# Gated outputs split where they are made, sigmoids loaded a job ahead, adaLN sums in another order, results stored one at a time

## The chip, the core and the metric

The kernel runs on one core of a Trainium2 chip. Its time is the device time in microseconds (us) of one execution. The engines that matter are TensorE (PE in the profile, with its weight loads as PEld), VectorE (DVE), ScalarE (ACT), GpSimd (POOL) and SyncE (SP). SP does no arithmetic: it issues every transfer between the chip's memory and the core's on-chip tiles, one after the other from one queue. A transfer that has to wait for its data holds all transfers behind it in that queue.

## The reference

One layer of a hybrid decoder block over 2048 tokens with 1024 channels, in fp32. What is computed:

```
ada = silu(c) @ w_ada + b_ada;  shift, scale, gate = split(ada)
h = rms_norm(x, g_pre) * (1 + scale) + shift
pv, pg, hq, hf, hi, hg, mg_pool, mg_hgrn = split(h @ w_in)        # 1024 -> 7168
P = per_group_linear(trailing_mean(pv) - pv) * pool_scale * silu(pg)   # 4 groups of 128 channels
A = P @ w_pool_o                                                      # 512 -> 1024
f = lb + (1 - lb) * sigmoid(hf);  q = silu(hq);  k = 1 - f;  v = hi
S_t = diag(f_t) S_(t-1) + k_t v_t^T;  o_t = S_t^T q_t                 # 8 heads of 128 channels
G = rms_norm(o, hgrn_norm_g) * silu(hg)
B = G @ w_hgrn_o                                                      # 1024 -> 1024
merged = sigmoid(mg_pool) * A + sigmoid(mg_hgrn) * B
out = x + gate * rms_norm(merged @ w_out, g_post)
```

P and G are the "gated outputs" of the title; the two sigmoids of the merge are the "sigmoids".

## The kernel before

**Products.** Every fp32 operand of a large matrix product is held as two fp32r tiles: hi is a cast of the value (ACT), lo is the value minus hi (DVE). A product is three matmuls, hi·hi, hi·lo and lo·hi (`three`, L275; all of them are recorded at L273). The helper that makes the two is `split` (L168, L169).

**Order of work.** The tokens are done in two passes of 1024, each as two halves t of 512. A pass is:
1. h, transposed to channels by tokens (`h_in`, L437), and the V projection in jobs (`v_job`, PSUM tiles psV). In pass 0 this is laced with the adaLN sums (`ada_sum`, L311: eight multiply-adds of w_ada tiles on DVE for each quarter q of the channels; `ada_done`, L325: a matmul with ones into psa, then shv and scv, the shift and scale of h).
2. Eight heads. In each, three quads of seven products (the tiles pa, pb, pe, pd) give f and q, the pool and the gate projections (gp), and the merge sigmoids (m). The recurrence of a head is a generator (`hgrn`) whose steps are dealt out between products by `tick`. Its end makes sgg, which is G of head h and half t (L697), and stores it to Gd in memory. `pg_got` makes spg, which is P of a group, and stores it to Pd. `m_got` stores the sigmoids to Sd.
3. The A stage: eight jobs (`a_job`, L811). Job j multiplies one weight item of w_pool_o with the four groups of P, for t = 0 and 1, into two PSUM tiles psA, and multiplies each with a sigmoid tile sm (the product is written into sm itself).
4. The B stage: eight jobs (`b_job`, L821), with two weight items each and the eight heads of G, into two tiles psB; again times sm, added, and split for the next product.
5. The Y stage: the output projection (`y_job`, tiles psy), the norm, and the results xr, which are stored to out. In pass 0 the x and h of pass 1 are made here.

**Where P and G come from.** In the kernel before `two_in` (L794) loads each half as one fp32 tile (P or G) and splits it there: Ph and Pl, Gh and Gl. The loads of P stand between products of the last head; those of G head j−1 stand ahead of A job j, and the last head's behind the last A job.

**Weights.** The weights are a list of items of 128 × 512, used in a fixed order. `take` (L263) hands out the next one and first prepares those up to four (LOOK) ahead: a raw load wr, a cast on ACT and a subtraction on DVE into a tile whl, and in pass 0 mostly a store of the split weights to scratch memory (scr), from which pass 1 and the later Y jobs load them whole (512 KB). There are four whl buffers, so the split of an item waits for TensorE to be through with the item four before it. There are four PSUM tiles for products, and an A or B job takes two.

**What sets the order.** The instructions of each engine stand in the order in which the scheduler of the framework puts them, by the program and by what each needs; an engine then runs its own in that order. `after` (L96) pins an instruction behind a given one; `gated` (L105) uses it to put a load behind the last store that was issued. `store` (L101) notes that store.

## Time and profile before

| | |
|---|---|
| median of 3 runs | 1894.23 us (1893.49 to 1901.12) |
| profiled execution | 1894.57 us, span 1892.8 us, mean granted TensorE clock 0.992 |
| instructions | 31547 |
| TensorE busy | 1815.8 us, 96% of the span |
| VectorE, ScalarE, GpSimd busy | 1104.8, 805.5 and 71.5 us (58%, 43%, 4%) |
| moved by transfers | 427.41 MB, mean 226 GB/s |

The span runs from the first to the last instruction; the profiled execution's own time is 1.8 us longer. In the profile, L12 is line 12 of the kernel before, `out<-in` names the tiles written and read, with the numbers of buffers left out, and an arrow behind an idle time names what ended it. The stages of pass 0 lie at about 28 to 86 us (first V jobs with the adaLN sums), to 160 (the other V jobs), to 704 (heads), 704.6 to 780.7 (A), to 877.7 (B) and to about 990 (Y); the A stage of pass 1 lies at about 1638 to 1701.6, its B stage behind it to about 1789.

### The profile page before, as it was taken

Reading aid. Unit: us, or ns where it says so; the run is one execution under the profiler, and the core shown is the slowest. Engines: PE = TensorE matmul, PEld = TensorE weight load, DVE = VectorE, ACT = ScalarE, POOL = GpSimd, SP = SyncE. Lnnn points to the kernel's source line nnn. Section 1 sums busy time; section 2 is a strip of 40 time slices with the busy share of each in tenths; the row PEclk is TensorE's granted clock in tenths of the full one; section 3 lists DMA queues with packets and bytes.
Section 4 is the critical chain, followed back from the end, with each engine's and each line's share of the span. In section 5 each row is a group of like instructions: output and inputs, shape, how many; then the busy total and the mean of one; then the engine's idle time right before and its main releaser. Section 6 shows DMA issues by size and latency. Waiting matters only on the chain.

```text
span 1892.8 us, 31547 instructions
## 1 busy us (share of the span) xinstructions
PE 1815.8 (96%) x12053; PEld 1461.7 (77%) x12053; DVE 1104.8 (58%) x2329; ACT 805.5 (43%) x1863; POOL 71.5 (4%) x136
## 2 busy tenths in 40 slices
PE   4999999999999998899999999999999999989997
PEld 3788888878888876677788778878878888778875
DVE  6567887887887884465533264554555556544322
ACT  3755656656656653223322344345344345321111
POOL 1100000000000000000000000000000000000000
PEclk9999999999999999999999999999999999999998
DMA  8698677576676677777887756565564564675475
GB/s 289 206 320 292 209 260 245 206 268 240 212 259 242 211 260 233 239 241 246 301 299 239 252 189 183 184 200 174 185 201 159 198 202 159 198 244 167 157 265 201
DMA packets 227314, 427.41 MB, mean 226 GB/s; under 512 B 17965, under 2 KB 108762, under 8 KB 227162
## 3 DMA queue, kind: packets, MB, share of 16 engines
q1 hardware_dynamic: 227162, 425.39, 66.7%
q8 instruction: 95, 1.56, 0.3%
q14 instruction: 57, 0.47, 0.1%
HBM read 261.22 MB, written 164.10 MB: 225 GB/s over the span
## 4 chain that ended last, share of the span: by engine, by line
PE 85%; DMA 5%; DVE 3%; ACT 2%; issue 1%; SPq 0%; POOL 0%; POOLq 0%; DVEq 0%; ACTq 0%
PE psB L273 9%; PE psV L273 7%; PE pam L273 7%; PE pagp L273 7%; PE pafq L273 7%; PE psy L273 7%; PE pegp L273 4%; PE pefq L273 4%; PE pem L273 4%; PE psa L273 4%; PE psA L273 3%; PE po L273 3%; PE pbfq L273 2%; PE pdfq L273 2%; PE pbm L273 2%; PE pbgp L273 2%
## 5 line engine op out<-in xcount | busy, mean ns | idle before, releaser
L169 DVE TENSOR_TENSOR whl<-wr,whl 128x512 fp32r<-128x512 f32 x210 | 145.1, 693 | 102.9 <-ACT whl L169 102.6
L574 DVE COPY_PREDICATED PT<-mask,psa 128x256 f32<-128x256 uint8 (+1 forms) x256 | 139.8, 546 | 54.1 <-PE psa L273 53.8
L273 PE MATMUL psB<-Gh,whl 128*128 128x512 f32 x512 | 161.7, 396 | 7.3 <-DVE sm L387 6.4
L169 ACT CAST whl<-wr 128x512 fp32r<-128x512 f32 x210 | 129.8, 621 | 88.8 <-PE psB L273 34.1
L273 PE MATMUL psy<-whl,mgh 128*128 128x512 f32 x512 | 161.1, 395 | 4.5 <-DMA whl<-scr_y 3.8
L273 PE MATMUL psV<-whl,hB 128*128 128x512 f32 x512 | 161.4, 397 | 1.0 <-ACT V L785 0.7
L273 PEld LDWEIGHTS psB<-Gh,whl 128*128 128x128 f32 x512 | 97.5, 191 | 30.1 <-DVE sm L387 7.6
L273 PEld LDWEIGHTS psy<-whl,mgh 128*128 128x128 f32 x512 | 96.0, 190 | 26.0 <-DMA whl<-scr_y 4.9
L273 PEld LDWEIGHTS psV<-whl,hB 128*128 128x128 f32 x512 | 96.5, 191 | 21.6 <-ACT V L785 0.9
L273 PE MATMUL psB<-Gl,whl 128*128 128x512 f32 x256 | 101.0, 396 | 0.0
L273 PE MATMUL psy<-whl,mgl 128*128 128x512 f32 x256 | 100.5, 392 | 0.0
L273 PE MATMUL psV<-whl,lB 128*128 128x512 f32 x256 | 100.2, 393 | 0.0
L273 PE MATMUL psA<-Ph,whl 128*128 128x512 f32 x256 | 87.7, 411 | 12.1 <-DVE sm L387 8.3
L273 PE MATMUL pam<-hT,whl 128*128 128x512 f32 x256 | 85.9, 396 | 0.0
L273 PE MATMUL pagp<-hT,whl 128*128 128x512 f32 x256 | 85.9, 396 | 0.0
L273 PEld LDWEIGHTS psa<-X,K 128*32 128x32 f32 x2816 | 52.7, 109 | 42.5 <-issue 28.6
L273 PE MATMUL pafq<-hT,whl 128*128 128x512 f32 x256 | 84.2, 389 | 0.0
L387 DVE TENSOR_TENSOR K<-K,TT 128x256 f32<-128x256 f32 x192 | 81.7, 425 | 0.6
L273 PE MATMUL psa<-X,K 128*32 128x48 f32 (+2 forms) x2816 | 70.1, 209 | 3.2 <-DVE PT L574 2.0
L387 DVE TENSOR_TENSOR y<-psy,gg 128x512 f32<-128x512 f32 x32 | 22.0, 689 | 83.4 <-ACT jy L882 83.2
L273 PEld LDWEIGHTS psA<-Ph,whl 128*128 128x128 f32 x256 | 49.2, 194 | 26.3 <-DVE sm L387 10.7
L882 ACT ACTIVATE jy<-psy 128x512 bf16<-128x512 f32 x32 | 19.1, 597 | 101.7 <-PE psy L273 100.7
(358 smaller groups left out, 4298.4 us busy)
## 6 DMA issues: line engine op xcount, KB each, us to landing
wr<-in_w_in_dram SPq DMA_DIRECT2D x122, 256.0 KB, 4.4
whl<-scr_y SPq DMA_DIRECT2D x48, 512.0 KB, 3.4
sm<-Sd SPq DMA_DIRECT2D x64, 256.0 KB, 4.7
whl<-scr_v SPq DMA_DIRECT2D x32, 512.0 KB, 4.7
wa<-in_w_ada_dram SPq DMA_DIRECT2D x32, 256.0 KB, 5.4
x<-in_x_dram SPq DMA_DIRECT2D x32, 256.0 KB, 4.7
Vd<-V SPq DMA_DIRECT2D x32, 256.0 KB, 2.4
scr_v<-whl SPq DMA_DIRECT2D x16, 512.0 KB, 2.8
```

Of the source, the lines that this page charges most:

```text
L169: return A.copy(hi, src32), V.tensor_tensor(lo, src32, hi.bitcast(F32), op=SUB)
L273: PE.matmul(o, lhsT=l, rhs=r, start=start, stop=stop, skip_group_check=True)
L387: return (e or V).tensor_tensor(o, a, b, op=op)
L574: V.copy_predicated(dst, m, src)
L882: A.activation(jy, pss[tk], AF.Square, scale=1.0 / 32, accum_out=rs[:, nn:nn + 1])
```

## The change

1. **Split where made.** `two_out` takes the place of the store of sgg and spg: it splits the tile at once, and stores the two parts as two transfers of 256 KB (Gd and Pd have room for both). `two_in` loads the two parts as two transfers and splits nothing. The last group of P (g = 3) and the last head of G (h = 7) aren't stored at all: their parts stay in on-chip tiles. So per pass 20 tiles are stored as 40 transfers, where 24 were stored as 24, and loaded as 40 in place of 24; SP has 64 transfers more in both passes.
2. **Sigmoids.** `sig_in` issues the loads of the next job's sm and hands out those that the job before it issued; the last A job issues the first of the B stage.
3. **adaLN.** All of the first quarter's sums are done, then `ada_done(0)` at once, ahead of `x_first`. `head_in(q)` begins with `ada_done(q)` and then does two sums of the next quarter, an `h_in`, two sums, an `h_in`, four sums; before, it was four sums, `ada_done`, two `h_in`, four sums.
4. **Results.** Results that wait to be stored are stored one at each `take`. Before, `flush_outs` stored all of them at the first items of a Y job or of the next pass.

The keys that `store` and `gated` are given are not used. The core of the diff:

```diff
-    def store(dst, src):
+    def store(key, dst, src):
         last["st"] = SP.dma_start(dst, src)
-        return last["st"]
...
     def take(look=LOOK):
+        if outs:
+            store("out", *outs.pop(0))
         i = state["use"]
...
-    def ada_sum(q, part, prev):
+    def ada_sum(q, k0, k1, prev):
...
-            for kk in range(4 * part, 4 * part + 4):
+            for kk in range(k0, k1):
...
-        V.scalar_tensor_tensor(scv[:, sl], scv[:, sl], 1.0, col("gpre")[:, sl], op0=ADD, op1=MUL)
-        return it
+        iv = V.scalar_tensor_tensor(scv[:, sl], scv[:, sl], 1.0, col("gpre")[:, sl], op0=ADD, op1=MUL)
+        return it, iv
...
         V.scalar_tensor_tensor(og, pot, col("ng"), og, op0=MUL, op1=MUL)
-        store(cx["Gd"][h][:, t, :], og)
+        two_out("G", p, h, t, og, cx, h == NH - 1)
...
         tt(sg, sg, cx["pw"].pop((g, t)))
-        store(cx["Pd"][g][:, t, :], sg)
+        two_out("P", p, g, t, sg, cx, g == NG - 1)
...
-        if t == grp == 0 and q == 1:
-            flush_outs()
...
-    def two_in(p, nm, i, src, cx, key):
-
+    def two_out(nm, p, i, t, src, cx, stay):
+
+        hi, lo = utile(f"{nm}h{p}_{i}_{t}", F32R), utile(f"{nm}l{p}_{i}_{t}", F32R)
+        split(src, hi, lo)
+        if stay:
+            cx["g" + nm][i, t] = (hi, lo)
+        else:
+            for z, w in enumerate((hi, lo)):
+                store((nm, i), cx[nm + "d"][i][:, t, z, :], w.bitcast(F32))
+
+    def two_in(nm, p, i, cx):
         for t in range(2):
-            f = utile(f"{nm}{p}_{i}_{t}")
-            gated(f, src[:, t, :])
-            hi, lo = utile(f"{nm}h{p}_{i}_{t}", F32R), utile(f"{nm}l{p}_{i}_{t}", F32R)
-            split(f, hi, lo)
-            cx[key][i, t] = (hi, lo)
+            cx["g" + nm][i, t] = tuple(utile(f"{nm}{z}{p}_{i}_{t}", F32R) for z in "hl")
+            for z, w in enumerate(cx["g" + nm][i, t]):
+                gated(w.bitcast(F32), cx[nm + "d"][i][:, t, z, :], (nm, i))
 
     def sig_in(p, j, w, cx):
+
+        nj, nw = (j + 1, w) if j + 1 < KT else (0, w + 1)
+        if (j, w) == (0, 0):
+            cx["sm"][j, w] = sig_load(p, j, w, cx)
+        if nw < 2:
+            cx["sm"][nj, nw] = sig_load(p, nj, nw, cx)
+        return cx["sm"].pop((j, w))
...
-        flush_outs()
         fin = p == NPASS - 1 and t == 1
...
-    it = ada_sum(0, 1, ada_sum(0, 0, None))
+    it = ada_sum(0, 0, KT, None)
+    with after(it):
+        it = ada_done(0)[1]
     with after(it):
         it = x_first(0, cxs[0], xss)
...
     def head_in(q):
-        if q < 3:
-            it = ada_sum(q + 1, 0, behind["v"])
-        with after(it if q < 3 else behind["v"]):
-            it = ada_done(q)
-            for k in (2 * q, 2 * q + 1):
-                ins = h_in(0, 0, k, cxs[0])
-        behind["a"] = ins[0]
-        behind["v"] = ada_sum(q + 1, 1, ins[1]) if q < 3 else ins[1]
+        it, iv = None, behind["v"]
+        if q:
+            with after(iv):
+                it, iv = ada_done(q)
+        for n, k in enumerate((2 * q, 2 * q + 1)):
+            if q < 3:
+                iv = ada_sum(q + 1, 2 * n, 2 * n + 2, iv)
+            with after(iv):
+                ia, iv = h_in(0, 0, k, cxs[0])
+        behind["a"] = ia
+        behind["v"] = ada_sum(q + 1, 4, KT, iv) if q < 3 else iv
         return it
...
-                        steps += [lambda g=g: two_in(p, "P", g, cx["Pd"][g], cx, "gP") for g in range(NG)]
+                        steps += [lambda g=g: two_in("P", p, g, cx) for g in range(NG - 1)]
...
             if j > 0:
-                two_in(p, "G", j - 1, cx["Gd"][j - 1], cx, "gH")
+                two_in("G", p, j - 1, cx)
             a_job(p, j, cx)
         while active:
             tick()
-        two_in(p, "G", NH - 1, cx["Gd"][NH - 1], cx, "gH")
```

Three places show what this does to the order of instructions. The rows name the line of the respective kernel, so L169 before is L171 in the change. First DVE at the start, before: the sums of quarter 1 (acc1 from the tiles wa1) and shv and scv of quarter 0.

```order
L169 TENSOR_TENSOR whl1_346<-wre1_240,whl1_346 128x512
L320 TENSOR_SCALAR acc1_349<-wa1_0_242,small_104 128x512
L322 SCALAR_TENSOR_TENSOR acc1_349<-wa1_1_244,small_104,acc1_349 128x512
L322 SCALAR_TENSOR_TENSOR acc1_349<-wa1_2_246,small_104,acc1_349 128x512
L322 SCALAR_TENSOR_TENSOR acc1_349<-wa1_3_248,small_104,acc1_349 128x512
L331 TENSOR_TENSOR shv_118<-psa_116,vec_102 128x2
L332 TENSOR_TENSOR scv_119<-psa_116,vec_102 128x2
L333 SCALAR_TENSOR_TENSOR scv_119<-scv_119,vec_102 128x2
L169 TENSOR_TENSOR lB110_0_369<-h32_0_0_0_366,hB110_0_368 128x512
L169 TENSOR_TENSOR lB210_0_380<-h32_0_0_1_377,hB210_0_379 128x512
L322 SCALAR_TENSOR_TENSOR acc1_349<-wa1_4_250,small_104,acc1_349 128x512
```

And in the change, where shv and scv (now L335 to L337) stand fourteen rows earlier, right behind quarter 0's last sum and ahead of the eight scalings of x:

```order
L326 SCALAR_TENSOR_TENSOR acc0_298<-wa0_7_220,small_104,acc0_298 128x512
L335 TENSOR_TENSOR shv_118<-psa_116,vec_102 128x2
L336 TENSOR_TENSOR scv_119<-psa_116,vec_102 128x2
L337 SCALAR_TENSOR_TENSOR scv_119<-scv_119,vec_102 128x2
L417 TENSOR_SCALAR x0_0_222<-x0_0_222,rst_147 128x512
```

Behind the scalings and the first two weight splits, the sums now stand between the lo parts of h:

```order
L171 TENSOR_TENSOR whl1_353<-wre1_240,whl1_353 128x512
L324 TENSOR_SCALAR acc1_356<-wa1_0_242,small_104 128x512
L326 SCALAR_TENSOR_TENSOR acc1_356<-wa1_1_244,small_104,acc1_356 128x512
L171 TENSOR_TENSOR lB110_0_367<-h32_0_0_0_364,hB110_0_366 128x512
L326 SCALAR_TENSOR_TENSOR acc1_356<-wa1_2_246,small_104,acc1_356 128x512
L326 SCALAR_TENSOR_TENSOR acc1_356<-wa1_3_248,small_104,acc1_356 128x512
L171 TENSOR_TENSOR lB210_0_380<-h32_0_0_1_377,hB210_0_379 128x512
```

So shv and scv no longer stand behind four sums, and no lB follows its neighbour directly. Second, DVE in the A stage of pass 0, before. The name sm0_2_0_1 is pass 0, job 2, w = 0 (the A stage), half 1; whl200 is the item of A job 0.

```order
L169 TENSOR_TENSOR whl206_8151<-wr206_8149,whl206_8151 128x512
L697 SCALAR_TENSOR_TENSOR sgg0_7_0_7546<-pot0_7_0_8174,vec_102,sgg0_7_0_7546 128x512
L387 TENSOR_TENSOR sm0_1_0_0_8006<-psA0_1_0_8010,sm0_1_0_0_8006 128x512
L387 TENSOR_TENSOR sm0_1_0_1_8008<-psA0_1_1_8024,sm0_1_0_1_8008 128x512
L169 TENSOR_TENSOR Gl0_1_0_8067<-G0_1_0_8064,Gh0_1_0_8066 128x512
L169 TENSOR_TENSOR Gl0_1_1_8073<-G0_1_1_8070,Gh0_1_1_8072 128x512
L169 TENSOR_TENSOR whl207_8216<-wr207_8214,whl207_8216 128x512
L387 TENSOR_TENSOR sm0_2_0_0_8083<-psA0_2_0_8087,sm0_2_0_0_8083 128x512
L387 TENSOR_TENSOR sm0_2_0_1_8085<-psA0_2_1_8123,sm0_2_0_1_8085 128x512
```

The same place in the change:

```order
L391 TENSOR_TENSOR sm0_2_0_0_8088<-psA0_2_0_8165,sm0_2_0_0_8088 128x512
L391 TENSOR_TENSOR sm0_2_0_1_8090<-psA0_2_1_8201,sm0_2_0_1_8090 128x512
L701 SCALAR_TENSOR_TENSOR sgg0_7_0_7647<-pot0_7_0_8248,vec_102,sgg0_7_0_7647 128x512
L171 TENSOR_TENSOR whl205_8156<-wr205_8154,whl205_8156 128x512
L171 TENSOR_TENSOR whl206_8225<-wr206_8223,whl206_8225 128x512
L171 TENSOR_TENSOR whl207_8289<-wr207_8287,whl207_8289 128x512
L391 TENSOR_TENSOR sm0_3_0_0_8161<-psA0_3_0_8234,sm0_3_0_0_8161 128x512
L391 TENSOR_TENSOR sm0_3_0_1_8163<-psA0_3_1_8265,sm0_3_0_1_8163 128x512
L171 TENSOR_TENSOR whl208_8346<-wr208_8344,whl208_8346 128x512
L171 TENSOR_TENSOR Gl0_7_0_8255<-sgg0_7_0_7647,Gh0_7_0_8254 128x512
```

The sm products of job 1 stood behind whl206 and now stand nine rows and more ahead of it; those of job 2 stood behind whl207 and now stand ahead of whl205. The Gl rows of the other heads are gone from here. Third, SP's queue in pass 1, where the recurrence of head 3 ends, before:

```order
L191 DMA whl381_13595<-scr_('m', 4)_2_4770 128x1024
L191 DMA whl382_13635<-scr_('m', 4)_3_4813 128x1024
L102 DMA Gd1_3_181<-sgg1_3_0_13371 128x512
L191 DMA whl383_13651<-scr_('m', 4)_4_4833 128x1024
L191 DMA whl384_13675<-scr_('m', 4)_5_4860 128x1024
```

And in the change:

```order
L193 DMA whl381_13693<-scr_('m', 4)_2_4820 128x1024
L193 DMA whl382_13738<-scr_('m', 4)_3_4868 128x1024
L106 DMA Gd1_3_181<-Gh1_3_0_13716 128x512
L106 DMA Gd1_3_181<-Gl1_3_0_13717 128x512
L193 DMA whl383_13754<-scr_('m', 4)_4_4888 128x1024
```

The load of whl383 stood behind one store, that of the finished tile, and now stands behind two, of which the second needs the subtraction. In the Y stage of pass 0, eight stores of xr stood in a row ahead of the loads of whl244 and those behind it; now one or two stores stand between two pairs of such loads.

More of the change, by code (lines that the diff above doesn't have):

```diff
@@ L99, in tile_block, with gated @@
     last = {"st": None}
-    def store(dst, src):
+    state = {"prep": 0, "use": 0}
+    outs = []
+    def store(key, dst, src):
         last["st"] = SP.dma_start(dst, src)
-        return last["st"]
-    def gated(dst, src):
+    def gated(dst, src, key=None):
         with after(last["st"]):
@@ L165, in tile_block @@
     ready = []
-    state = {"prep": 0, "use": 0}
     def split(src32, hi, lo):
@@ L186, in keep @@
             scr[key] = dram("scr_" + "_".join(map(str, key)), [P, 2 * T])
-            store(scr[key], w.bitcast(F32))
+            store(key, scr[key], w.bitcast(F32))
     def again(key, name):
@@ L309, in tile_block @@
     accs = {}
-    def ada_sum(q, part, prev):
-        if part == 0:
+    def ada_sum(q, k0, k1, prev):
+        if k0 == 0:
             accs[q] = utile(f"acc{q}")
@@ L366, in gate_out @@
         V.tensor_tensor(bg, gp, bg, op=MUL)
-        store(ggd[n], bg)
+        store("gg", ggd[n], bg)
     S = [cst.tile([P, P], F32, name=f"S{h}") for h in range(NH)]
@@ L752, in m_got @@
         A.activation(s, u, AF.Sigmoid)
-        store(cx["Sd"][j, row][:, t, :], s)
+        store(("Sd", j, row), cx["Sd"][j, row][:, t, :], s)
     def v_job(p, t, grp, q, cx, hook=None):
@@ L785, in v_job, with sig_load @@
             A.copy(vt, pss[tk])
-            store(cx["Vd"][:, t * NT + tk, grp * T:(grp + 1) * T], vt)
+            store("Vd", cx["Vd"][:, t * NT + tk, grp * T:(grp + 1) * T], vt)
     def v_head(p, h, cx):
         vt = vp.tile([P, 8, P], F32, tag="v", name=f"V{p}_{h}")
-        gated(vt, cx["Vd"][:, :, h * P:(h + 1) * P])
+        gated(vt, cx["Vd"][:, :, h * P:(h + 1) * P], "Vd")
         cx["V"][h] = vt
-    def two_in(p, nm, i, src, cx, key):
-        for t in range(2):
-            f = utile(f"{nm}{p}_{i}_{t}")
-            gated(f, src[:, t, :])
-            hi, lo = utile(f"{nm}h{p}_{i}_{t}", F32R), utile(f"{nm}l{p}_{i}_{t}", F32R)
-            split(f, hi, lo)
-            cx[key][i, t] = (hi, lo)
-    def sig_in(p, j, w, cx):
+    def two_out(nm, p, i, t, src, cx, stay):
[7 more added lines that the diff above has]
+    def two_in(nm, p, i, cx):
+        for t in range(2):
+            cx["g" + nm][i, t] = tuple(utile(f"{nm}{z}{p}_{i}_{t}", F32R) for z in "hl")
+            for z, w in enumerate(cx["g" + nm][i, t]):
+                gated(w.bitcast(F32), cx[nm + "d"][i][:, t, z, :], (nm, i))
+    def sig_in(p, j, w, cx):
+        nj, nw = (j + 1, w) if j + 1 < KT else (0, w + 1)
[4 more added lines that the diff above has]
+        return cx["sm"].pop((j, w))
+    def sig_load(p, j, w, cx):
         r = []
@@ L806, in sig_in @@
             s = utile(f"sm{p}_{j}_{w}_{t}")
-            gated(s, cx["Sd"][j, w][:, t, :])
+            gated(s, cx["Sd"][j, w][:, t, :], ("Sd", j, w))
             r.append(s)
@@ L826, in b_job @@
             for t in range(2):
-                three(ps[t], w, [cx["gH"][4 * half + i, t] for i in range(4)], half == 0, half == 1)
+                three(ps[t], w, [cx["gG"][4 * half + i, t] for i in range(4)], half == 0, half == 1)
         for t in range(2):
@@ L840, in gg_in @@
             g = utile(f"gg{p}_{n}")
-            gated(g, ggd[n])
+            gated(g, ggd[n], "gg")
             cx["gg"].append(g)
-    outs = []
-    def flush_outs():
-        while outs:
-            store(*outs.pop(0))
     def y_job(p, t, nn, q, cx):
@@ L902, in y_job @@
                 if fin:
-                    store(*o)
+                    SP.dma_start(*o)
                 else:
@@ L909, in tile_block @@
     for p in range(NPASS):
-        cx = {k: {} for k in ("F", "Q", "G", "V", "pw", "Gd", "Pd", "Sd", "gP", "gH", "a", "mg", "x", "xc", "h32",
+        cx = {k: {} for k in ("sm", "F", "Q", "G", "V", "pw", "Gd", "Pd", "Sd", "gP", "gG", "a", "mg", "x", "xc", "h32",
                               "mv", "y", "yss")}
@@ L913, in tile_block @@
         for h in range(NH):
-            cx["Gd"][h] = dram(f"Gd{p}_{h}", [P, 2, T])
+            cx["Gd"][h] = dram(f"Gd{p}_{h}", [P, 2, 2, T])
         for g in range(NG):
-            cx["Pd"][g] = dram(f"Pd{p}_{g}", [P, 2, T])
+            cx["Pd"][g] = dram(f"Pd{p}_{g}", [P, 2, 2, T])
         for j in range(KT):
```

## The prediction

> **What bounds the kernel now.** I read the profile's page first, then the engine shares by stretch of the run, then what TensorE waited for, then the order in time where it waited.
>
> ```profile
> PE 1815.8 (96%) x12053; PEld 1461.7 (77%) x12053; DVE 1104.8 (58%) x2329; ACT 805.5 (43%) x1863; POOL 71.5 (4%) x136
> PE 85%; DMA 5%; DVE 3%; ACT 2%; issue 1%; SPq 0%; POOL 0%; POOLq 0%; DVEq 0%; ACTq 0%
> ```
>
> The first row gives busy time by engine, the second the chain that ended last. The matmuls are 96% of the span and the change takes none of them away, so all that can be won is in the 1892.8 − 1815.8 = 77 us in which TensorE stood idle, and in the stretches where its clock was below 1. The table by stretch shows where that is. Its columns: stretch, length, busy time (count) of PE, PEld, DVE, ACT and POOL, granted clock, DMA share, GB/s.
>
> ```profile
> 10.00:30.00 20.00, 7.15 (x23) 4.71 (x24) 12.84 (x25) 10.02 (x23) 4.44 (x8) 1.00 1.06 380
> 30.00:60.00 30.00, 25.93 (x125) 20.75 (x124) 22.33 (x42) 11.21 (x19) 0.00 (x0) 0.94 0.55 187
> 160.00:690.00 530.00, 529.33 (x4195) 427.71 (x4194) 432.08 (x958) 317.90 (x766) 25.02 (x42) 1.00 0.68 236
> 690.00:720.00 30.00, 26.31 (x280) 18.90 (x278) 19.68 (x46) 13.03 (x27) 0.00 (x0) 1.00 0.86 278
> 720.00:780.00 60.00, 49.70 (x216) 37.90 (x216) 25.52 (x45) 20.54 (x54) 3.50 (x6) 0.94 0.68 228
> 780.00:880.00 100.00, 95.66 (x400) 77.03 (x401) 59.92 (x92) 20.93 (x35) 0.41 (x2) 0.97 0.71 240
> 1070.00:1600.00 530.00, 526.87 (x4106) 424.94 (x4105) 280.55 (x679) 228.74 (x569) 15.61 (x26) 1.00 0.58 187
> 1640.00:1700.00 60.00, 54.67 (x311) 42.19 (x309) 26.98 (x51) 18.36 (x50) 2.40 (x4) 1.00 0.68 219
> ```
>
> The long stretches 160–690 and 1070–1600 are the eight heads of each pass: TensorE idles 0.67 and 3.13 us there, so nothing is to be won, only lost. The idle time lies at the start (10–60), in the A stage of pass 0 (690–780: 3.69 + 10.30), in its B stage (780–880: 4.34) and in the A stage of pass 1 (5.33). What it waited for (total, times, longest):
>
> ```profile
> PE psa L329 <- DVE acc L322: 12.9, 4, 9.4
> PE psA L273 <- DVE sm L387: 8.3, 7, 2.0
> PE psB L273 <- DVE sm L387: 6.4, 3, 2.7
> PE psy L273 <- DMA whl<-scr_y: 3.8, 3, 2.8
> PE psA L273 <- ACT Ph L169: 3.7, 5, 1.6
> ```
>
> **The start.** In order of time (start, length, instruction, idle before it):
>
> ```profile
> 22.14 1.29 DVE L169 TENSOR_TENSOR whl<-wre,whl 128x512 fp32r<-128x512 f32 x2
> 23.34 0.48 DVE L320 TENSOR_SCALAR acc<-wa,small 128x512 f32<-128x512 f32 x1
> 23.86 2.33 DVE L322 SCALAR_TENSOR_TENSOR acc<-wa,small,acc 128x512 f32<-128x512 f32 x3
> 26.61 0.78 ACT L443 ACTIVATE h<-xT,shv,scv 128x512 f32<-128x512 f32 x1 [5.75 <-DVE scv L333]
> 28.09 1.22 PE L273 MATMUL psV<-whl,hB 128*128 128x512 f32 x2
> 49.03 0.69 DVE L169 TENSOR_TENSOR lB<-h,hB 128x512 fp32r<-128x512 f32 x1 [1.56 <-ACT hB L169]
> 54.13 1.05 PE L329 MATMUL psa<-one,acc 128*128 128x1 f32 x8 [1.63 <-DVE acc L322]
> ```
>
> Today the first h waits on ACT until scv is done at 26.5, because scv stands on DVE behind four sums of the next quarter (0.48 + 2.33). In the change shv and scv come before x is even scaled, so h waits only for x's transposes, which follow the last x scaling (it ends where the whl row begins, 22.1). I put their end at 22.6; h costs 0.78 and its cast 0.62: the first V matmul at about 24.1, 4 us earlier than 28.09. After that VectorE paces the quarters: eight sums, two lB, two whl and the closing adds (0.5 by the gap between the end of the third sum, 26.2, and h at 26.61) are 0.48 + 7 × 0.78 + 4 × 0.69 + 0.5 = 9.2 us, beside about 1.56 + 0.64 of waiting for hB, a gap that the change fills with sums. That would shorten the three quarters too, but each still ends on a sum that psa waits for (the 1.63), so I keep the 4: **−4, bounds 0 and −6** (what the two 1.63 and part of the hB gaps would add, less what the later quarters wait for loads).
>
> **The A stage of pass 0.** This is the largest term. One turn of it:
>
> ```profile
> 733.14 0.69 DVE L169 TENSOR_TENSOR whl<-wr,whl 128x512 fp32r<-128x512 f32 x1 [1.92 <-ACT whl L169]
> 735.25 1.28 DVE L387 TENSOR_TENSOR sm<-psA,sm 128x512 f32<-128x512 f32 x2
> 735.98 0.50 PE L273 MATMUL psA<-Ph,whl 128*128 128x512 f32 x1 [1.01 <-DVE sm L387]
> 715.75 0.32 SPq L102 DMA_DIRECT2D Sd<-sgm  x1
> 716.16 0.88 SPq L108 DMA_DIRECT2D P<-Pd  x2
> 719.24 0.62 ACT L169 CAST Ph<-P 128x512 fp32r<-128x512 f32 x1 [3.51 <-DMA P<-Pd]
> ```
>
> An A job takes two PSUM banks of four, so job j needs the banks that the sm products of job j−2 release. In DVE's order before, the weight split that needs the buffer of job j (whl206: item 6, four buffers, so job 2's) stands ahead of the sm products of job j−1 (sm0_1). TensorE finishes job 2, ACT casts, DVE splits at 733.14, only then come sm0_1 at 735.25 and job 3 at 735.98: TensorE stops once a job. In the change sm0_0 to sm0_2 stand ahead of whl205, and the split that needs job 3's buffer (whl207) stands ahead of sm0_3, which job 5 needs, with a whole job between. So the cycle of stops opens. The lower three rows are the other wait: the last P goes out and back through memory and then through ACT; now its parts stay on chip, and the fourteen Gl and eight Pl subtractions and the same casts are gone from the stage. What could be got is the idle 3.69 + 10.30 and, at clock 0.94, 6% of 60 us = 3.6: 17.6. Some waits stay, since TensorE also runs the last head's recurrence here, whose own steps wait on DVE and ACT. **−13, bounds 0 and −17.6.** The added cost is memory traffic: P and G come back as two parts of 256 KB instead of one. By the order, 22.5 MB lie between the first P load and the last of G6 (21.0 before; pass 1: 20.2, was 16.5). The first P load was issued at 695, and at the start's 380 GB/s 22.5 MB take 59 us, at the stage's present 254 GB/s 89 us:
>
> ```profile
> 695.00:760.00 65.00, 55.56 (x357) 41.47 (x355) 31.92 (x62) 23.63 (x56) 2.30 (x4) 0.97 0.77 254
> ```
>
> At share 0.77 that is 254 / 0.77 = 330 GB/s full, an estimate: 68 us, so G6 would come at about 763. With 13 us won the B stage begins at 780.7 − 13 = 767.7. It fits, with 5 us to spare. SP issues 76 transfers in that time, at 0.44 (half of 0.88, the P row) 33 us. This is where the sum is weakest.
>
> [...]
>
> **The B stage of pass 0, and A of pass 1.**
>
> ```profile
> 780.73 0.50 PE L273 MATMUL psB<-Gh,whl 128*128 128x512 f32 x1 [2.04 <-DVE sm L387]
> 790.35 0.83 SPq L108 DMA_DIRECT2D G<-Gd  x1
> 791.23 4.85 SPq L108 DMA_DIRECT2D wg<-in_w_ada_dram  x8
> 796.42 0.73 PE L273 MATMUL psB<-Gh,whl 128*128 128x512 f32 x2 [0.85 <-ACT Gh L169]
> 1694.00 0.38 SPq L108 DMA_DIRECT2D G<-Gd  x1
> ```
>
> The last G is stored, reloaded (790.35, 1694.00) and split before the second half of job 0; now it stays. The sm products lose their splits in front and are loaded a job ahead. The idle 4.34 plus 3% of clock (2.9) is 7.2; the wg loads and gate sums stay, so **−5, bounds 0 and −7.2**. In pass 1 weights come already split, the idle is 5.33: **−4, bounds 0 and −5.3**.
>
> **The results.**
>
> ```profile
> 928.45 7.04 SPq L102 DMA_DIRECT2D out_dram<-xr  x8
> 1839.74 19.73 SPq L191 DMA_DIRECT2D whl<-scr_y  x8
> ```
>
> Eight stores held SP for 7.0 us with weight loads behind them, and at 1839.74 too the loads stood behind such stores. One store per item lets loads pass between. The psy row gives the limit, 3.8: **−3, bounds 0 and −3.8.** A store whose xr is not ready still holds SP, but only one load waits behind it.
>
> **The heads, where the cost goes.** Per pass 22 tiles (eight of P, fourteen of G) get a cast on ACT and a subtraction on DVE here, and the 20 of them that leave the chip get two stores instead of one.
>
> ```profile
> L169 DVE TENSOR_TENSOR whl<-wr,whl 128x512 fp32r<-128x512 f32 x210 | 145.1, 693 | 102.9 <-ACT whl L169 102.6
> L169 ACT CAST whl<-wr 128x512 fp32r<-128x512 f32 x210 | 129.8, 621 | 88.8 <-PE psB L273 34.1
> SPq L102 <- DVE sgg L697: 39.1, 25, 2.8
> whl<-scr_v SPq DMA_DIRECT2D x32, 512.0 KB, 4.7
> ```
>
> 22 × 0.693 = 15.2 us on DVE, which is 82% busy in 160–690 (432.08 of 530), and 22 × 0.621 = 13.7 us on ACT (60%). It fits in the averages. On SP the queue stands at the first part's store until the cast is done and at the second's until the subtraction: 0.62 + 0.69 = 1.31 us more than today's wait for sgg, whose longest is 2.8: 4.1. Behind it stand weight loads and, in pass 0, raw loads and scratch stores. A pass has 168 items in about 604 us of heads, 3.6 us each; a load is issued three items ahead, 10.8, and needs 4.7: about 6 us are spare, so 4.1 is covered. If nothing covered it, 40 × 1.31 = 52 us would be lost. I take two uncovered tiles, **+2.5, bounds 0 and +52**, near the lower end since today's waits of the same kind left 0.67 us of idle in pass 0. Loading sigmoids earlier takes two more tiles and moves a load past one job's other loads: at nothing, inside the traffic above.
>
> **Sum.** −4 − 13 − 5 − 4 − 3 + 2.5 = −26.5. The profiled execution took 1894.57 (span 1892.8 and 1.8 around it), 0.3 over the median, so about **1868**.
>
> **Rivals.**
> 1. *The A stage becomes bound by its transfers.* For it: the bytes above, and each transfer is issued from one queue in order, so a store that waits (Sd, scr_a) stops the loads. Against it: the 380 row. If the stage gets no more than its 254 GB/s, the last G6 part comes at 695 + 89 = 784, later than 780.7, and the 13 are gone: 1881.
> 2. *The stops move and don't go.* If sm still comes behind a split that waits for TensorE, or bunched raw loads come late for it, A and B win nothing (22 back): 1890. For it: DVE's order still mixes the two. Against: the one job between.
> 3. *Slower: SP held at the split stores.* Place: the heads; price: 1.31 us for each of the 40 tiles where loads have no slack, 52 in place of 2.5: 1918. It eats all other gains (29) from 0.73 us per tile. For it: pass 1 already idles 3.13 in its heads. Against: the 6 us spare.
> 4. *Everything goes.* All bounds of gain: −6 − 17.6 − 7.2 − 5.3 − 3.8 = −39.9: 1855.
>
> **How the numbers follow.** Forecast 0.60 (alone 1860 to 1877), rival 1 0.18, rival 2 0.08, rival 3 0.07, rival 4 0.07. Half a per cent, 9.5 us, is about what a measurement of this kernel tells from no change. The forecast, rival 4 and most of rival 1 (0.16) are faster by more: 0.83. Rival 2 and the rest of 1 (0.02), less 0.01 for rival 2 on the other side, are no change: 0.09. Slower: 0.08. The range 1855 to 1887 leaves out rival 3, most of rival 2 and half of rival 4: about 0.18.
>
> **What would show it.** Right: the first V matmul near 24 us; psA no longer waiting for sm, and A jobs some 6 us apart; no G reload ahead of B; PE idle in the heads within 3 us of the 0.67 and 3.13; DMA share in the A stage near 0.9. Wrong: waits for P or sm by DMA in the A stage (rival 1), psA or psB still waiting for DVE sm (2), new waits for whl or wr in the heads with SP standing at Gd or Pd stores (3).

## The result, and the profile after

The changed kernel took 1842.37 us (median of 4 runs, 1841.64 to 1846.02) against 1894.56 us of the kernel before beside it (4 runs): a ratio of 0.9721, 95% interval 0.9696 to 0.9747. The prediction was 1868, with a range from 1855 to 1887. The sign was right, the gain of 52 us was twice the 26.5 of the sum, and the time lies below the range.

The page of the changed kernel, busy time:

```profile
span 1841.2 us, 31695 instructions
PE 1797.7 (98%) x12053; PEld 1458.0 (79%) x12053; DVE 1103.1 (60%) x2329; ACT 807.5 (44%) x1863; POOL 71.1 (4%) x136
```

TensorE's idle time fell from 77.0 to 1841.2 − 1797.7 = 43.5 us. That is 33.5 of the 51.6 us. The other 18.1 us are *busy* time: the same 12053 matmuls took 1797.7 us instead of 1815.8. The prediction had said that all that can be won lies in the idle time and in stretches of low clock, and had priced the second with 6.5 us.

The stages, each from its first matmul to the first of the next, in both profiled executions (us), with what the prediction's sum had for them:

| stage | before | changed | difference | predicted |
|---|---|---|---|---|
| start, to the first psV | 28.1 | 23.7 | −4.4 | −4 |
| V, pass 0 | 108.0 | 108.2 | +0.2 | |
| heads, pass 0 | 568.5 | 568.7 | +0.2 | +2.5 with pass 1 |
| A, pass 0 | 76.1 | 54.9 | −21.2 | −13 |
| B, pass 0 | 96.8 | 89.1 | −7.7 | −5 |
| Y, pass 0 | 99.3 | 98.2 | −1.1 | −3 with pass 1 |
| V, pass 1 | 89.2 | 88.7 | −0.5 | |
| heads, pass 1 | 572.2 | 570.5 | −1.7 | |
| A, pass 1 | 63.4 | 53.5 | −9.9 | −4 |
| B, pass 1 | 87.2 | 87.0 | −0.2 | |
| Y, pass 1, to the end | 104.0 | 98.7 | −5.3 | |

The same by busy time, clock and transfers, in the table by stretch (columns as in the prediction). First three stages of the kernel before, A and B of pass 0 and A of pass 1:

```profile
704.60:780.70 76.10, 61.41 (x319) 45.61 (x317) 34.58 (x65) 25.17 (x64) 3.50 (x6) 0.96 0.70 230
780.70:877.50 96.80, 93.16 (x389) 74.95 (x390) 57.04 (x87) 20.03 (x33) 0.41 (x2) 0.96 0.74 247
1638.20:1701.60 63.40, 56.46 (x319) 43.33 (x317) 29.67 (x56) 19.10 (x52) 2.40 (x4) 1.00 0.68 221
```

And the same three of the changed kernel:

```profile
700.60:755.50 54.90, 53.71 (x319) 43.50 (x317) 22.02 (x45) 14.06 (x44) 3.27 (x6) 1.00 0.98 357
755.50:844.60 89.10, 89.10 (x390) 72.96 (x390) 56.60 (x86) 19.30 (x33) 0.41 (x2) 1.00 0.86 293
1602.00:1655.50 53.50, 52.86 (x318) 43.45 (x317) 19.84 (x40) 8.68 (x33) 2.40 (x4) 1.00 1.00 363
```

In A of pass 0 the 319 matmuls are the same, the idle time went from 14.7 to 1.2, and the busy time from 61.4 to 53.7. TensorE's clock is whole, and the transfer engines now work at 0.98. What TensorE waited for in that stage, before:

```profile
PE psA L273 <- DVE sm L387: 5.1, 4, 2.0
PE psA L273 <- ACT Ph L169: 2.6, 3, 1.6
PE psB L273 <- DVE sm L387: 2.0, 1, 2.0
PE pot L695 <- ACT on L689: 2.0, 2, 1.0
PE pd L273 <- ACT KS L662: 1.2, 1, 1.2
PE po L273 <- DVE SC L672: 0.6, 1, 0.6
```

And in the changed kernel, all that is left:

```profile
PE psA L277 <- DMA Ph<-Pd: 0.6, 1, 0.6
PE psa L277 <- DVE PT L578: 0.3, 1, 0.3
PE psA L277 <- DMA Pl<-Pd: 0.3, 1, 0.3
```

Not only the sm and Ph waits are gone, but also those of the recurrence (on, KS, SC), which the prediction had expected to stay.

### The profile page after: what moved, and what is told of

The parts are those of the page before. It is cut to its first block, busy times and chain, and to the rows that moved or that the text cites. A ratio compares the mean times of both kernels' runs of the same rounds, so it can differ in the third digit from the quotient of the medians.

```text
span 1841.2 us, 31695 instructions
## 1 busy us (share of the span) xinstructions
PE 1797.7 (98%) x12053; PEld 1458.0 (79%) x12053; DVE 1103.1 (60%) x2329; ACT 807.5 (44%) x1863; POOL 71.1 (4%) x136
## 4 chain that ended last, share of the span: by engine, by line
PE 90%; DMA 2%; DVE 2%; ACT 1%; issue 1%; SPq 0%; POOL 0%; POOLq 0%; DVEq 0%; ACTq 0%
PE psB L277 9%; PE psV L277 8%; PE psy L277 8%; PE pagp L277 7%; PE pafq L277 7%; PE pam L277 7%; PE pegp L277 5%; PE pefq L277 5%; PE psA L277 5%; PE pem L277 4%; PE psa L277 4%; PE po L277 3%; PE pbfq L277 3%; PE pbgp L277 2%; PE pdfq L277 2%; PE pdgp L277 2%
## 5 line engine op out<-in xcount | busy, mean ns | idle before, releaser
L171 DVE TENSOR_TENSOR whl<-wr,whl 128x512 fp32r<-128x512 f32 x210 | 144.8, 691 | 97.6 <-ACT whl L171 93.4
L171 ACT CAST whl<-wr 128x512 fp32r<-128x512 f32 x210 | 129.8, 621 | 103.5 <-issue 25.2
L277 PE MATMUL psA<-Ph,whl 128*128 128x512 f32 x256 | 83.3, 398 | 1.0 <-DMA Ph<-Pd 0.9
L171 ACT CAST mgh<-sm 128x512 fp32r<-128x512 f32 x32 | 19.7, 621 | 122.1 <-DVE sm L391 122.1
```

Of the source, the lines that this page charges most:

```text
L171: return A.copy(hi, src32), V.tensor_tensor(lo, src32, hi.bitcast(F32), op=SUB)
L277: PE.matmul(o, lhsT=l, rhs=r, start=start, stop=stop, skip_group_check=True)
```

## The experiments

Two theories were set against each other for the A and B stages. S: the splits of P and G, taken off ScalarE and VectorE there, opened the stops. L: loading the sigmoids a job earlier did it. For the size of the gain: E, a stop of TensorE costs more than the idle time shown; I, the idle time is its whole price. In the ratios below each kernel stands against the kernel before on the same chip; the changed kernel's own is 0.9721, and 0.9726 (0.9697 to 0.9754) when it was run a second time.

**Sigmoids in their own job again.**

```diff
     def sig_in(p, j, w, cx):
...
-        if nw < 2:
-            cx["sm"][nj, nw] = sig_load(p, nj, nw, cx)
-        return cx["sm"].pop((j, w))
+        return sig_load(p, j, w, cx)
```

> The changed kernel with the sigmoids loaded in their own job again, all else as changed. Theory S (the splits of P and G, taken out of the A and B stages, opened the stops): A of pass 0 stays below 58 us (54.9 changed, 76.1 before), A of pass 1 below 56, the time is 1842 to 1848. Rival L (the sigmoids loaded a job ahead did it, since the product with sm is what TensorE waited for): A of pass 0 is 65 us or more, the time 1860 or more.

Measured: 1845.22 us, 0.9732 (0.9713 to 0.9751). A of pass 0 is 57.7 us, of pass 1 54.0. One wait for sm came back:

```profile
PE psA L277 <- DVE sm L391: 2.0, 1, 2.0
```

S holds, L falls. The total isn't told from the changed kernel's; the stage shows some 2.7 us, and without its change the changed kernel has 54.9 and, run a second time, 55.3.

**Splits where they are read again.** `two_out` stores the whole tile, `two_in` loads and splits it, the last ones too.

```diff
     def two_out(nm, p, i, t, src, cx, stay):
-        hi, lo = utile(f"{nm}h{p}_{i}_{t}", F32R), utile(f"{nm}l{p}_{i}_{t}", F32R)
-        split(src, hi, lo)
...
+        store((nm, i), cx[nm + "d"][i][:, t, :], src)
...
     def two_in(nm, p, i, cx):
         for t in range(2):
...
+            f = utile(f"{nm}{p}_{i}_{t}")
+            gated(f, cx[nm + "d"][i][:, t, :], (nm, i))
+            hi, lo = utile(f"{nm}h{p}_{i}_{t}", F32R), utile(f"{nm}l{p}_{i}_{t}", F32R)
+            split(f, hi, lo)
+            cx["g" + nm][i, t] = (hi, lo)
```

> The changed kernel with P and G stored whole and split where they are read again, the last ones too; sigmoids still a job ahead. Theory S: A of pass 0 is 68 us or more, A of pass 1 59 or more, B of pass 0 93 or more, the time 1865 to 1880. Rival L: A of pass 0 below 60, the time 1842 to 1852. If each part opens only some of the stops, both this kernel and the one with sigmoids in their own job lie between.

Measured: 1867.13 us, 0.9843 (0.9829 to 0.9858). A of pass 0 is 70.9, A of pass 1 60.1, B of pass 0 91.8. S holds here too, except that B gave back 2.8 of its 7.7 us instead of 4. What TensorE waited for in A of pass 0:

```profile
PE pd L277 <- ACT KS L666: 3.7, 1, 3.7
PE psA L277 <- ACT Ph L171: 3.1, 4, 1.7
PE po L277 <- DVE SC L676: 1.9, 2, 1.1
PE pot L699 <- ACT on L693: 1.0, 1, 1.0
PE psA L277 <- DVE sm L391: 0.9, 1, 0.9
```

The order in time at the longest of them shows what the prediction had not seen. SP issues the load, ScalarE's queue holds the cast, and the copy KS of the recurrence, which needs no load at all, stands behind it and a weight cast:

```profile
744.71 0.38 SPq L111 DMA_DIRECT2D G<-Gd  x1
749.04 0.62 ACT L171 CAST Gh<-G 128x512 fp32r<-128x512 f32 x1 [6.09 <-DMA G<-Gd]
749.57 0.61 ACT L171 CAST whl<-wr 128x512 fp32r<-128x512 f32 x1
750.09 0.58 ACT L666 COPY KS<-pk 128x512 f32<-128x512 f32 x1
750.72 2.08 PE L277 MATMUL pd<-V,KS 128*128 128x128 f32 x8 [3.68 <-ACT KS L666]
```

ScalarE stood for 6.1 us at a cast whose result nobody needs before the B stage, and TensorE for 3.7 us at what came after it.

**Both back.** The two edits above together, so that only the adaLN order and the stores of results remain of the change.

> The changed kernel with both the splits back at the load and the sigmoids in their own job; only the adaLN order and the stores of results stay changed. With e1 and e2 it fills a two by two table. If the two parts of the change add up, the loss in A of pass 0 is 2.7 + 16.0 = 18.7 us over the changed kernel (73.6) and the time about 1870. If sigmoids ahead are worth more when splits stand in the way: A of pass 0 is 76, A of pass 1 63, B of pass 0 95 or more, the time 1876 to 1885.

Measured: 1886.67 us, 0.9943 (0.9923 to 0.9963), above both forecasts. A of pass 0 is 79.7, of pass 1 64.6, B of pass 0 96.5. The parts don't add up:

| A of pass 0 and of pass 1, us | sigmoids in their own job | a job ahead |
|---|---|---|
| split where read | 79.7 and 64.6 | 70.9 and 60.1 |
| split where made | 57.7 and 54.0 | 54.9 and 53.5 |

In pass 1, where the clock is 1.00 in all four, loading ahead is worth 4.5 us beside late splits and 0.5 beside early ones. In pass 0 it is worth 8.8 and 2.8, but the clock has a part in that: A of pass 0 ran at 0.89 in the kernel with both back, at 0.95 in the one that splits where it reads and at 1.00 in the two others, which is 8.5, 3.4 and 0 us. TensorE's idle time there is 15.3, 11.3, 3.4 and 1.2 us in the order of the table, so that in idle time loading ahead is worth 4.0 and 2.2. Either part removes some of the same stops, so that an experiment that undoes one alone understates it: the waits of psA for sm are 8.4 us over the whole run here, 1.2 with the sigmoids a job ahead alone, 2.0 with the early splits alone, and none with both. L falls as the account of the whole gain, but not for these waits.

**The last ones stored and loaded too.** `two_out` is called with `stay` false, `two_in` for all groups and heads, with the parts still split where made.

> The changed kernel, but the last group of P and the last head of G are stored as two parts and loaded again as well, like the others. If keeping them on chip matters (in the kernel before, the last P went out and back while TensorE stopped for 0.74 us at its cast, and the last G 0.85): both A stages are 2 to 5 us longer than 54.9 and 53.5, psA waits for Ph or Pl by transfer at the fourth group of job 0, the time 1845 to 1850. If a transfer without a cast behind it comes in time anyway: 1842 to 1844.

Measured: 1849.12 us, 0.9754 (0.9725 to 0.9782); the interval overlaps the changed kernel's 0.9726 on the same chip. By stage: A of pass 0 57.7 (55.3 in the changed kernel run beside it), B of pass 0 91.0 (89.0), A of pass 1 55.4 (53.5), about as expected. The expected wait for a transfer in A isn't there, though: in A of pass 0 TensorE waits for Ph and Pl by transfer for 0.8 us, in the changed kernel for 0.9, and the new stop in that stage is one of 0.8 us at KS. The waits over the whole run have a new one within B:

```profile
PE psB L277 <- DMA Gh<-Gd: 1.5, 1, 1.5
```

**The old adaLN order.** `ada_sum`, `ada_done` and `head_in` as before.

> The changed kernel with the adaLN sums in the order of before. If the sums' order is worth only the start: the first V matmul at 28.1 us instead of 23.7, every later stage as long as in the changed kernel, the time 1846.5. If it is worth more (later quarters pace too): 1849 or more. If the V jobs behind absorb it: 1842 to 1843.

Measured: 1848.8 us, 0.9746 (0.9731 to 0.9761). The first V matmul comes at 27.7 us, and all stages from the heads on are within 1.0 us of the changed kernel's. The V stage took 109.5 there, but it also took between 106.5 and 109.7 us in the kernels whose start is the changed one, so the 2 us over the expected 1846.5 aren't assigned. By the ratio alone, this kernel and the next aren't told from the changed one; what tells is the place.

**Results in bursts again.** `flush_outs` at its two old places.

> The changed kernel with the results stored in bursts again. If the bursts hold up the weight loads: the waits of psy for scr_y weights come back (3.6 us in Y of pass 1), Y of pass 1 is 102 to 104 instead of 98.7, the time 1845 to 1848. If the gain in the Y stage comes from elsewhere (the B stage in front of it): 1842 to 1843.

Measured: 1847.43 us, 0.9742 (0.9727 to 0.9756). Y of pass 0 is 101.7 us (98.2), of pass 1 100.3 (98.7), and the wait is back, though less than in the kernel before:

```profile
PE psy L279 <- DMA whl<-scr_y: 1.6, 2, 1.4
```

Y of pass 1 is below the 102 to 104 expected, and its length alone shows nothing, since the changed kernel had 100.1 there when it was run a second time. What shows that the bursts hold up the loads is where the wait of 1.4 us stands, 56 us into the stage; the 2.8 us of the kernel before stood 58 us into it. The kernel with both back, which keeps the new stores, has 98.9 there, against 104.0 of the kernel before.

**The price of a stop.** One PSUM tile for all sixteen halves of an A stage, so that TensorE has to wait for each sm product.

```diff
         sm = sig_in(p, j, 0, cx)
+        if j == 0:
+            cx["psA"] = bank(f"psA{p}")
         for t in range(2):
-            ps = bank(f"psA{p}_{j}_{t}")
+            ps = cx["psA"]
```

> The changed kernel with one PSUM tile for all A jobs, so that TensorE stops for the sm product behind each of the 16 halves of an A stage. It measures what a stop costs. Theory E (a stop costs more than the idle time that the trace shows: the matmuls at its edges take 0.15 us more before and 0.11 after, and a stage with many stops runs below full clock): each A stage grows by the added idle plus 16 x 0.26 = 4 us or more. Rival I (the idle time is the whole price, as the prediction's bounds took it): each stage grows by the added idle within 1 us. Idle added: about 16 stops of 1 us in each stage, the time about 1842 + 2 x 20 = 1882 by E, 1874 by I.

Then the same with three copies of the PSUM tile ahead of the product:

```diff
+            for _ in range(3):
+                V.tensor_copy(utile(f"jA{p}_{j}_{t}_{_}"), ps)
             tt(sm[t], ps, sm[t])
```

> The same with three copies of the PSUM tile on VectorE ahead of each sm product (their results are not used), so that each of the 16 stops is about 2 us longer. By theory E with a fixed price of edges, the growth over the added idle stays 4 us per stage, as with short stops, unless the clock falls: then it is more, and the granted clock of the stage shows it (0.95 and a growth of 8 us or more). By rival I, the growth equals the added idle and the clock stays 1.00.

Measured: 1871.14 us (0.9879, 0.985 to 0.9908) and 1919.2 us (1.0127, 1.0102 to 1.0152). The tiles that were left free let some matmuls of the B stage run between the A jobs, so there are fewer stops than sixteen (four and five more than in the changed kernel, counting those above 0.15 us; with the copies fifteen and eleven more), and A and B must be taken together. The total of 1871 lies below both forecasts, 1882 and 1874, which had sixteen. The column on the clock is at most what the clock cost, since the mean also counts the time in which TensorE stood idle. Against the changed kernel (144.0 us for A and B of pass 0, 140.6 of pass 1):

| | growth | idle added | 1 − clock, times length of A, added | left |
|---|---|---|---|---|
| one tile, pass 0 | 12.6 | 8.2 | 1.6 | 2.8 |
| one tile, pass 1 | 14.3 | 7.0 | 3.2 | 4.1 |
| and three copies, pass 0 | 38.8 | 24.8 | 11.7 | 2.3 |
| and three copies, pass 1 | 37.6 | 24.4 | 12.2 | 1.0 |

The A stages of the second of them, where the clock is 0.84:

```profile
698.70:771.70 73.00, 49.59 (x244) 37.06 (x242) 34.83 (x66) 10.50 (x30) 2.08 (x4) 0.84 0.72 242
1639.10:1715.30 76.20, 51.36 (x254) 38.90 (x253) 33.27 (x63) 8.41 (x32) 2.40 (x4) 0.84 0.53 186
```

I falls: the growth exceeds the idle time by 4 to 14 us, not by 1. E holds in kind, not in its size for each stage. At 0.26 us a stop, the added stops make 1.0, 1.3, 3.9 and 2.9 us in the order of the table: 9.1 in all against 10.2 left, though the single rows don't agree. With long stops most of the surcharge is the clock, as the expectation's second branch had it.

**Each tile split twice.** Behind the first split the parts are added up again and split a second time, before they are stored. What is computed stays the same.

```diff
         split(src, hi, lo)
+        tt(src, hi.bitcast(F32), lo.bitcast(F32), op=ADD)
+        split(src, hi, lo)
         if stay:
```

> The changed kernel with each gated output split, put together again and split a second time before its parts are stored: one cast and two VectorE operations more for each of 24 tiles a pass, and SP stands about 2 us longer at each pair of stores. It measures how much cover the heads have. Theory C (loads issued three items ahead have some 6 us to spare, and VectorE and ScalarE have room): the heads grow by less than 3 us in each pass, the time stays below 1849. Rival H (SP held at the stores reaches TensorE, the slower case of the prediction): about 2 us for each of 20 stored tiles, 40 us in each pass, or at least 10.

Measured: 1846.34 us, 0.9737 (0.9712 to 0.9762), not told from the changed kernel. The heads took 569.4 and 571.1 us (568.7 and 570.5). Two stretches of 530 us in the heads of each pass, with the operations that were added (in the changed kernel VectorE was busy for 441.61 and 298.17 us in them):

```profile
160.00:690.00 530.00, 528.24 (x4245) 426.33 (x4243) 460.26 (x1013) 340.22 (x805) 27.70 (x42) 1.00 0.69 243
1040.00:1570.00 530.00, 527.34 (x4122) 425.52 (x4124) 320.70 (x745) 252.74 (x611) 15.63 (x26) 1.00 0.59 196
```

VectorE at 87% in pass 0 still keeps TensorE at 528.2 of 530. So VectorE and ScalarE have the room that C says. H isn't tested by it, because SP did not stand longer at the stores of the parts. SP's waits there were, in the kernel before (its other row, 39.1 for sgg, is in the prediction) and then in the changed kernel:

```profile
SPq L102 <- DVE spg L387: 26.4, 13, 3.1
SPq L106 <- ACT Gh L171: 30.4, 15, 2.7
SPq L106 <- ACT Ph L171: 9.7, 6, 2.9
SPq L106 <- DVE Gl L171: 6.9, 21, 0.5
```

With 2.9 us for Pl, that is 65.5 us before and 49.9 in the changed kernel, and the same rows add up to 40.1 with each tile split twice.

**More traffic in the A stage.** One load more of 256 KB for each half of each G head, 3.7 MB a pass.

```diff
                 gated(w.bitcast(F32), cx[nm + "d"][i][:, t, z, :], (nm, i))
+            if nm == "G":
+                gated(utile(f"dup{p}_{i}_{t}"), cx[nm + "d"][i][:, t, 0, :], (nm, i))
```

> The changed kernel with one more load of 256 KB for each half of each G head in the A stages (fourteen a pass, 3.7 MB; what is loaded isn't used). It measures how near the A stage is to being bound by its transfers, where the share of the transfer engines is 0.98 and 1.00 in the changed kernel. If the stage is at the limit (357 GB/s): A of each pass grows by 3.7 MB / 357 GB/s = 10 us, with waits for sm, whl or wr by transfer, the time about 1862. If the transfers still have slack, so that only TensorE sets the pace: less than 2 us in each, 1842 to 1846.

Measured: 1851.51 us, 0.9768 (0.9735 to 0.9801). A of pass 0 grew by 6.8 us, from 54.9 to 61.7, A of pass 1 by 0.9. A stretch of A of pass 0, and A of pass 1:

```profile
700.00:755.00 55.00, 50.79 (x323) 40.56 (x311) 20.92 (x42) 11.69 (x34) 2.07 (x4) 0.97 1.01 364
1609.50:1664.00 54.50, 52.78 (x319) 43.48 (x317) 17.98 (x38) 8.70 (x33) 2.40 (x4) 1.00 1.04 400
```

Both forecasts missed in pass 0, and the premise of the first is wrong: 357 GB/s is not what the stage can reach at most, since A of pass 1 went from 363 to 400 with the added loads and so took most of them in. At 400 the 3.7 MB are 9 us, an estimate, of which pass 0 hid 2 to 3. So the first of the prediction's rivals was near: A of pass 0 is a few us from being bound by its transfers. The added loads also stand in SP's queue, which no run separates from their bytes.

**The changed kernel once more.**

> The changed kernel itself, on the same chip as the two others, as their measure: 1842, ratio 0.972.

Measured: 1843.81 us, 0.9726 (0.9697 to 0.9754).

## Why the prediction was right in kind and wrong in size

**The start** (−4): right. The first h runs at 22.13 and the first V matmul at 23.7, which had been put at 24.1:

```profile
22.13 0.78 ACT L447 ACTIVATE h<-xT,shv,scv 128x512 f32<-128x512 f32 x1 [1.81 <-PE xT L445]
23.73 2.06 PE L277 MATMUL psV<-whl,hB 128*128 128x512 f32 x4
```

As argued, the later quarters gave nothing that shows (V of pass 0: 108.0 and 108.2, in a stage that varies by 3 us).

**A of pass 0** (−13, bound −17.6; measured −21.2). Two steps failed. The first is "Some waits stay, since TensorE also runs the last head's recurrence here, whose own steps wait on DVE and ACT". The waits for on, KS and SC, 3.8 us, were taken for the recurrence's own. They came from what stood ahead of its steps in the queues of ScalarE and VectorE. In the kernel before, on and KS stood behind a weight cast that waited for TensorE to be through with the buffer, and SC behind a split of G that waited for its load (KS, then SC):

```profile
751.19 0.62 ACT L169 CAST whl<-wr 128x512 fp32r<-128x512 f32 x1 [2.84 <-PE psA L273]
751.72 0.58 ACT L662 COPY KS<-pk 128x512 f32<-128x512 f32 x1
759.24 0.69 DVE L169 TENSOR_TENSOR Gl<-G,Gh 128x512 fp32r<-128x512 f32 x1 [4.91 <-ACT Gh L169]
759.85 0.34 DVE L672 SCALAR_TENSOR_TENSOR SC<-S,TT,pd 128x128 f32<-128x128 f32 x1
```

In the changed kernel KS still comes right behind such a weight cast and a split, at 737.2, but TensorE gets to the matmuls that need it only at 741.2. That the late splits of P and G are the cause is shown by the kernels that put them back, where these waits are back too; why the steps come in time without them is not shown. Keeping these waits took 4.6 us off the bound without cause. The second is the bound itself, "the idle 3.69 + 10.30 and, at clock 0.94, 6% of 60 us". It took busy time for work. But a stop has edges, which the profile books as busy. One stop, in the order in time of the kernel before:

```profile
741.37 0.39 PE L273 MATMUL psA<-Ph,whl 128*128 128x512 f32 x1
741.79 0.62 ACT L169 CAST whl<-wr 128x512 fp32r<-128x512 f32 x1 [2.15 <-PE psA L273]
742.44 0.69 DVE L169 TENSOR_TENSOR whl<-wr,whl 128x512 fp32r<-128x512 f32 x1 [2.08 <-ACT whl L169]
743.05 1.28 DVE L387 TENSOR_TENSOR sm<-psA,sm 128x512 f32<-128x512 f32 x2
743.79 0.69 PE L273 MATMUL psA<-Ph,whl 128*128 128x512 f32 x1 [2.04 <-DVE sm L387]
744.28 0.63 PE L273 MATMUL psA<-Pl,whl 128*128 128x512 f32 x1
744.71 1.06 PE L273 MATMUL psA<-Ph,whl 128*128 128x512 f32 x2
```

The rows of ACT and DVE bear out the prediction's account of these stops: the weight split waits for TensorE, and the sm products stand behind it. No load is waited for at this one. In a stream one matmul starts 0.227 us after another, though each is recorded with 0.39. The one before the stop starts 2.42 us ahead of the next: 2.04 idle, 0.227 its turn, and 0.15 booked as busy because nothing overlaps its end. At an ordinary stop the first one after it takes 0.11 longer (0.50 instead of 0.39, as at 735.98 in the prediction's rows). That is 0.26 for each of 13 stops (two short ones aren't in the list above), 3.4 us. Idle 13.5, clock 4% of 76.1 = 3.0, edges 3.4 make 19.9 of the 21.2.

**A of pass 1** (−4, bound −5.3; measured −9.9). The same two steps, in a stage that showed a clock of 1.00. Idle fell by 6.3 (from 6.9, over the whole stage and not the 60 us of the window that the bound was read from), edges of six stops are 1.6, and 2.0 us of busy time aren't accounted for; the small matmuls of the recurrence are among them.

**B of pass 0** (−5, bound −7.2; measured −7.7). The term kept 2.2 us back for wg loads and gate sums. They stopped nothing: the stage has no idle time left and a clock of 1.00.

**Results** (−3, bound −3.8; measured −6.4, 5.3 of it in pass 1). The mechanism was right, since the bursts bring a wait back at the same place. The bound had the idle time alone. In pass 1 it is 3.8 (14.4 to 10.6), and the stop that ends at 1846.4 is followed by a stretch at half pace, some 1.7 (of the kind shown in the last section).

**Heads** (+2.5): nothing was lost; V and heads together gained 1.8. The step that failed here is "1.31 us more than today's wait" for each tile: SP stood at these stores for less time than before, not more (49.9 us against 65.5). So the 6 us of cover (worked out from 604 us of heads, which are 568.5 in the table of stages) weren't called on, and no run here tests them; why SP stood for less stays open.

**The rivals.** The fit of the transfers had been put at 5 us to spare; the added loads point to 2 to 3. The full rate had been estimated at 330 GB/s from the share; the stage ran at 357, and at its end at 408 (last section). The stops didn't move (1890): neither psA nor psB waits for sm any more. Slower through SP (1918): no trace of it. "Everything goes" (1855) was nearest, and still 13 us too slow, since its bounds held the idle time and little else (6.5 us for the clock, nothing for the edges).

Over the whole run, what a kernel has more than the changed kernel (span 1841.2, idle 43.5):

| kernel | span more | idle more | ratio |
|---|---|---|---|
| before | 51.6 | 33.5 | 1.54 |
| both back | 44.9 | 26.4 | 1.70 |
| split where read | 25.9 | 16.4 | 1.58 |
| one tile | 24.8 | 14.1 | 1.76 |
| one tile, three copies | 74.7 | 48.4 | 1.54 |

The five are those that differ by more than 20 us; of the others, which differ by less than 10, the ratio lies anywhere between 1.0 and 2.3. Of the 18.1 us of busy time that went, the two causes named here make up most: the changed kernel has none of the five stretches at half pace that the last section lists (5 × 1.7 = 8.5), and 25 stops above 0.15 us instead of 48 (23 × 0.26 = 6.0). The rest, 3.6, stays open.

Had the sum counted all the idle time in A, B and Y as removable (3.69 + 10.30 + 4.34 + 5.33 + 3.8 = 27.5) and multiplied it by 1.6, it would have come to −44 there and −48 with the start, an estimate made with these results in hand.

## What to carry to other kernels

An operation that waited, for a load or for a buffer, stopped what stood behind it on its engine here (with the splits where they are read, a cast stood 6.1 us for its load, and TensorE then 3.7 us for a copy behind that cast), so look in its queue for what stands behind such a wait and not only for who needs its result; doing the conversion where the data is made took the wait for the load out of ScalarE's queue altogether (41.1 us for P and G between 700 and 785 us in the kernel before, none in the changed one). Where the busiest engine stops and starts, its idle time can be less than what can be won: here, over the larger differences, each us of it cost 1.5 to 1.8. And when a transfer doubles for it, compare the bytes of that one stage with the rate that it can reach, since here the stage had only 2 to 3 us to spare.

## What the runs showed of the hardware

**Behind some 2 us of idle time in 3.4 us, TensorE ran at half pace for the next 3.4.** After the stop quoted above, from 743.79 to 747.27, matmuls start 0.43 us apart instead of 0.227. The granted clock before and after, there and at the stop that ends at 771.47, and around one of 1.44 us in pass 1 that has no such stretch behind it:

```profile
740.51:743.92 3.41, 1.38 (x7) 0.83 (x6) 1.48 (x3) 1.14 (x2) 0.00 (x0) 1.00 0.22 85
743.92:747.33 3.41, 3.41 (x9) 2.67 (x10) 1.01 (x2) 0.00 (x0) 0.00 (x0) 0.50 1.01 321
767.82:771.23 3.41, 1.23 (x5) 0.55 (x4) 2.24 (x4) 2.17 (x6) 0.00 (x0) 1.00 0.47 190
771.23:774.64 3.41, 3.17 (x8) 2.49 (x9) 1.38 (x3) 0.09 (x1) 0.00 (x0) 0.50 0.91 274
1692.84:1696.25 3.41, 2.04 (x9) 1.67 (x10) 2.51 (x4) 0.62 (x1) 0.00 (x0) 1.00 0.75 237
1696.25:1699.67 3.42, 3.42 (x17) 2.76 (x15) 0.00 (x0) 0.05 (x1) 0.00 (x0) 1.00 0.80 250
```

Such stretches begin near the stops at 743.8, 771.5, 780.7, 808.3 and 1846.4, each worth some 1.7 us. In the traces of the two kernels the record of the clock has two values, 1.00 and 0.50, and its changes lie whole multiples of 3.413 us apart: the five stretches are 3.413 us long each and begin at 743.92, 771.23, 781.47, 808.78 and 1846.43, which are 8, 3, 8 and 304 times 3.413 us apart. Each kernel has one more of this length near its start, at 44.19 in the kernel before and at 49.55 in the changed one, and their last 8.8 and 6.5 us are at 0.50 too. With the run laid out in windows of 3.413 us from one such change to the next, the idle time of TensorE in a window goes with the clock in the one behind it better than the length of one stop does: the window ahead of 771.23 has a stop of 0.98 and part of one of 1.44, and 2.18 us of idle time in all, while the stop of 1.44 in pass 1 stands alone in its window, with 1.37. From where the record of the clock begins, at 30.54 and 29.07 us, the two traces have seven windows at full clock with 1.95 us of idle time or more, and each was followed by one at half clock; of five windows between 1.5 and 1.95 it was two, of 1053 below 1.5 it was none. What sets the clock is not shown beyond that.

**The transfers moved more than the 330 GB/s that the prediction had estimated as their full rate.** The end of A in the changed kernel:

```profile
740.00:756.00 16.00, 16.00 (x85) 13.40 (x85) 6.44 (x12) 4.16 (x15) 1.20 (x2) 1.00 1.05 408
```

That is 408 GB/s over 16 us, with TensorE never idle. With the added loads, A of pass 1 moved 400 over its 54.5 us. The most that this core can move is not shown.
